# A hybrid decoder layer on one core: a new front, modulation rows as a list, and a new last output column

## The chip, the core and the metric

The kernel runs on one core of a Trainium2 chip. The metric is the device time of one execution in microseconds (us). The median of three runs of the kernel before is 730.69 us (729.06 to 731.81). The profile is that of a further execution, which took 731.29 us.

## The reference, cut to what matters

The layer takes x (512 tokens by 2048 features) and a conditioning vector c. From c it makes a modulation vector of 3 x 2048 numbers: shift, scale and gate. These two lines are what the change is about:

```python
mod = silu(c) @ w_ada + b_ada;  shift, scale, gate = split(mod, 3)
h = rms_norm(x) * (1 + scale) + shift          # 512 x 2048
proj = h @ w_in                                # 4160 columns
y = concat([rg_lru(...) * silu(gr), attention(...) * silu(ga)])
out = x + gate * (y @ w_out)                   # 2048 columns
```

All is in float32. The recurrent branch and the attention between `proj` and `y` aren't touched by the change.

## The kernel before, in words

Everything is kept with features on the 128 partitions and the 512 tokens along a row. So h is 16 tiles `h0` to `h15` of 128 x 512, one for each 128 features; the scale and the shift of a tile are a column `mod[:, 16 + k]` and a column `mod[:, k]`.

A float32 product is made of three products of rounded parts: every weight and every h is split into a high part (rounded, on ScalarE) and a low part (the rest, on VectorE), and TensorE multiplies high by high, high by low and low by high (`mm3s`, `mm_hi`, `mm_lo`; every such product is recorded at line 125). `wload` loads a group of weights and splits it into `whi` and `wlo`.

The modulation. A row of w_ada (one column of `mod` for 128 features: 128 x 2048 numbers, 1 MB) is loaded as a tile `ada`, multiplied by silu(c), which stands in every partition (`cb`), and summed along the row by one VectorE instruction (`ttr`, L276). So each h needs two such sums, of its scale row `16 + k` and of its shift row `k`, and then a multiplication by the scale and the norm (`x`, L102), the rounded h (ScalarE or L114) and its low part (L102).

The front (L220 to L465). x is loaded a second time by tokens in eight pieces of 512 KB (`xtok`) for the squares (ScalarE, `sqj`) and, through TensorE transposes, for the first two tiles of x. Ahead of the eighth piece stand the small table `vec` and the scale row of h0 (1 MB, row 16). Then the norm `rx` is made by small VectorE steps and spread over all partitions by four products on TensorE (`rb_ps`). TensorE multiplies a constant tile `junk` in between (`warm`). `make_h(0)` and `make_h(1)` follow, with their other rows in pieces of 256 or 512 KB, and the weights of the first eight output columns (`wfraw`, `wfs`), which `proj_first` multiplies: 24 products with `h0`, then 24 with `h1`.

The input projection (L528 to L546). The 16 tiles of h are cut into chunks of 2, 3, 4 and 7 (`CHUNKS`). For each of the first three chunks the loop goes over all output columns in groups of 4, 2 and 2 (`GROUP`; 128 features a column): load and split the weights, multiply, and put the sums into a `pj` tile, by ScalarE in the first chunk and added by VectorE in the others. After the first eight columns the first chunk has six groups of 24 products; the second chunk has 16 groups of 18, the third 16 of 24; a narrow column for the rotary key (`proj_kr`) stands in the middle of each. The loop draws the next chunk's h from a generator `hgen`, evenly over its groups: 6, 8 and 14 row sums in the first three chunks. A scheduler orders the instructions of VectorE, ScalarE and TensorE; the loads on SP go out in the order of the code, and each engine keeps its order.

The end. The output projection makes 16 columns of 512 tokens from 16 tiles of y in pieces of four tiles (`oproj`). The last column (`order[-1]`) is made in two halves of 256 tokens throughout, so that the first half can leave while the second is multiplied. `ofin` multiplies the sum by the gate and adds x (`xo`). The gate rows are summed by `gate`, called through `gates`.

Of the kernel before, what the change touches and what calls it, by code (L numbers as in the profile page):

```python
# [33 lines left out]
GROUP = (4, 2, 2, 1)  # L34
MORDER = tuple(range(8)) + tuple(range(20, 24)) + tuple(range(16, 20)) + tuple(range(8, 16)) + tuple(range(24, 32))
# [3 lines left out]
NB0 = 0  # L39
NB1 = 1  # L40
P0 = 8
XA = 7
SETUP = (0, 2)
WARM = (4, 6, 4, 14)
# [40 lines left out]
def body(ctx, nc, tc, a):  # L85
# [38 lines left out]
    def mm(out, lhsT, rhs, start, stop, **kw):  # L124
        PE.matmul(out=out, lhsT=lhsT, rhs=rhs, start=start, stop=stop, **kw)  # L125
# [95 lines left out]
    DMA.dma_start(out=c4, in_=a["c"])  # L221
    id4 = p1.tile([4, 4], F32, name="id4")
# [13 lines left out]
    tab(c4, c4, AF.Silu)  # L236
    split(ch, cl, c4)
# [141 lines left out]
    ada0 = [ada(16, (2, 2)), ada(0, (2, 1, 1))]  # L379
    KT0 = CHUNKS[0][1]  # L380
    NG = NF // 4
    wfs = {(k, n): bigt(4 + k * NG + n, "wfs", F32R) for k in range(KT0) for n in range(NG)}
    wfraw = {kn: pjt(16 + i, F32, "wfraw") for i, kn in enumerate(wfs)}

    def wf_load(k, n):
        raw = wfraw[k, n]
        DMA.dma_start(out=raw, in_=a["winf"][k, n])
        act(wfs[k, n][:, 0], raw, AF.Copy)
# [31 lines left out]
    warm(WARM[3])  # L420

    def make_h(k):
        if k >= KT0:
            xload(k)
        parts = (2, 2) if k < KT0 else (4,)
        if k:
            yield from ada(16 + k, parts)
        x = xt[k]
        if k == 0:
            next(ada0[1])  # L430
            next(ada0[1])
            stt(x, x, mod[:, 16:17], rb_ps, ALU.mult, ALU.mult)
            act(rb, rb_ps, AF.Copy)
            yield from ada0[1]
        else:
            yield from ada(k, parts)
            stt(x, x, mod[:, 16 + k:17 + k], rb, ALU.mult, ALU.mult)
        t = bigt(k, f"h{k}", F32R)
        hh[k], hl[k] = t[:, 0], t[:, 1]
        if k < KT0:  # L440
            ts(hh[k], x, mod[:, k:k + 1], None, ALU.add)
        else:
            act(hh[k], x, AF.Identity, bias=mod[:, k:k + 1])
        i = stt(hl[k], x, mod[:, k:k + 1], hh[k].bitcast(F32), ALU.add, ALU.subtract)
        if k < KT0:
            mark[0] = ins_of(i)

    run(make_h(0))
    wf_load(0, 1)
    los = iter(range(NG))  # L450
    for i, _ in enumerate(make_h(1)):
        if i >= NB0:
            with tc.issue_after(ins_of(ttr_last[0])):
                for n in itertools.islice(los, NB1):
                    wf_lo(0, n)
    for n in los:
        with behind():
            wf_lo(0, n)
# [4 lines left out]
    DMA.dma_start(out=row[:, :R_ID], in_=a["row"][:, :R_ID])  # L463
    DMA.dma_start(out=row[:, R_MK:], in_=a["row"][:, R_MK:])
    DMA.dma_start(out=pos_i, in_=a["pos"])  # L465
# [37 lines left out]
    def proj_first(ms):  # L503
        k0, kc = CHUNKS[0]
        ps = [bank("mm" if n < 6 else "aux", "pp") for n, m in enumerate(ms)]
        for k in range(k0, k0 + kc):
            for i, (w, h) in enumerate(((0, hh), (0, hl), (1, hh))):
                for n, m in enumerate(ms):
                    mm(ps[n], wfs[k, n // 4][:, w, (n % 4) * P:(n % 4 + 1) * P], h[k], k == k0 and i == 0, k == k0 + kc - 1 and i == 2)
        for n, m in enumerate(ms):  # L510
            evac(0, m, ps[n])
# [17 lines left out]
    for ci in range(LC):  # L529
        nk0, nkc = CHUNKS[ci + 1]  # L530
        hgen = itertools.chain.from_iterable(make_h(k) for k in range(nk0, nk0 + nkc))
        done = 0
        ng = 32 // GROUP[ci]
        g0 = NF // GROUP[ci] if ci == 0 else 0
        if ci == 0:
            proj_first(MORDER[:NF])
        for g in range(g0, ng):
            while done < 2 * nkc * (g + 1 - g0) // (ng - 1 - g0):
                next(hgen, None)
                done += 1  # L540
            if g == (g0 + ng) // 2:
                proj_kr(ci)
            proj_group(ci, g)
        run(hgen)
# [385 lines left out]
    def oproj(m, k0, k1, first, last, kind="oa"):  # L930
        halves = m == order[-1]
        if first:
            if halves:
                for i in range(2):
                    ops[m, i] = bank(kind, "oa")
            else:
                ops[m] = bank(kind, "oa")
        wh, wl = wload(a["wout"][m][:, k0 * P:k1 * P], (k1 - k0) * P)
        xs = [(yh[k], yl[k]) for k in range(k0, k1)]
        if halves:  # L940
            for i, t in enumerate(HV):
                mm3s(ops[m, i][:, t], wh, wl, [(xh[:, t], xl[:, t]) for xh, xl in xs], first, last)
        else:
            mm3s(ops[m], wh, wl, xs, first, last)
# [159 lines left out]
    for n, m in enumerate(order):  # L1104
# [3 lines left out]
        if m not in acc and m not in half:  # L1108
            ks = [(0, 4), (4, 8)] + ks
        for k0, k1 in ks:  # L1110
# [4 lines left out]
        while gated[0] < 2 * n + 2:  # L1115
            gates(32)
# [8 lines left out]
def _layout(x, c, positions, w_ada, b_ada, w_in, conv_w, conv_b, w_rg_a, b_rg_a, w_rg_x, b_rg_x, lru_lambda,  # L1125
# [6 lines left out]
    d["c"] = con(c).reshape(4, S)  # L1132
    d["pos"] = con(positions[0].reshape(NT, P).T)
# [60 lines left out]
```

## Time and profile before

| what | us |
|---|---|
| median of 3 runs | 730.69 |
| the profiled execution | 731.29 |
| its span in the trace | 729.5 |
| TensorE busy / VectorE / ScalarE | 718.4 / 527.1 / 353.6 |
| first product of h0, of h1, of the first weight group behind them | 26.79, 35.11, 40.65 |
| mean granted TensorE clock | 0.998 |

The span is from the first to the last record of the profiled execution, and 1.8 us of its time lie around it. An engine's idle time costs something only where the last work waits for it.

### The profile page before, as it was taken

Reading aid. Unit: us, or ns where it says so; the run is one execution under the profiler, and the core shown is the slowest. Engines: PE = TensorE matmul, PEld = TensorE weight load, DVE = VectorE, ACT = ScalarE, POOL = GpSimd, SP = SyncE. Lnnn points to the kernel's source line nnn. Section 1 sums busy time; section 2 is a strip of 40 time slices with the busy share of each in tenths; the row PEclk is TensorE's granted clock in tenths of the full one; section 3 lists DMA queues with packets and bytes.
Section 4 is the critical chain, followed back from the end, with each engine's and each line's share of the span. In section 5 each row is a group of like instructions: output and inputs, shape, how many; then the busy total and the mean of one; then the engine's idle time right before and its main releaser. Section 6 shows DMA issues by size and latency. Waiting matters only on the chain.

```text
span 729.5 us, 10070 instructions
## 1 busy us (share of the span) xinstructions
PE 718.4 (98%) x3625; PEld 597.0 (82%) x3626; DVE 527.1 (72%) x949; ACT 353.6 (48%) x728; POOL 29.4 (4%) x34
## 2 busy tenths in 40 slices
PE   9799999999999999999999999999999999999998
PEld 4588888788788888888888888888888887888887
DVE  2997888799998889888765566567686786783232
ACT  7376322231323479884545568677565533222221
POOL 0000000000000000001011111111120100000000
PEclk9999999999999999999999999999999999999999
DMA  8998376996922422223243315113333795984420
GB/s 306 392 404 332 116 255 224 360 329 251 355 80 55 141 91 77 76 89 102 83 134 94 90 63 202 60 58 116 130 120 132 228 297 188 312 269 166 118 93 29
DMA packets 46001, 127.94 MB, mean 175 GB/s; under 512 B 5372, under 2 KB 9340, under 8 KB 42368
## 3 DMA queue, kind: packets, MB, share of 16 engines
q1 hardware_dynamic: 38896, 106.34, 42.3%
q10 hardware_dynamic: 7056, 20.97, 8.4%
q8 instruction: 28, 0.46, 0.3%
q14 instruction: 21, 0.17, 0.1%
HBM read 123.10 MB, written 4.19 MB: 174 GB/s over the span
## 4 chain that ended last, share of the span: by engine, by line
PE 82%; DMA 8%; DVE 7%; issue 2%; SPq 1%; ACT 0%; DVEq 0%
PE pp L125 35%; PE oa L125 24%; DMA ada<-in_ada 4%; PE sc L125 4%; PE uwuv L125 3%; PE uwqn L125 3%; PE uwuk L125 3%; DVE ada L276 3%; PE op L125 2%; PE uqp L125 2%; DMA xtok<-in_xtok 1%; DVE wlo L118 1%; DVE pj L118 1%; PE tp L896 1%; DMA wfraw<-in_winf 1%
## 5 line engine op out<-in xcount | busy, mean ns | idle before, releaser
L125 PE MATMUL pp<-h,whi 128*128 128x512 f32 x992 | 241.8, 391 | 0.5 <-ACT h L90 0.5
L90 ACT ACTIVATE whi<-wraw 128x512 fp32r<-128x512 f32 (+4 forms) x172 | 126.7, 740 | 209.3 <-PE oa L125 68.4
L125 PEld LDWEIGHTS pp<-h,whi 128*128 128x128 f32 x992 | 184.9, 188 | 39.7 <-issue 0.9
L118 DVE TENSOR_TENSOR wlo<-wraw,whi 128x512 fp32r<-128x512 f32 (+4 forms) x172 | 141.0, 822 | 66.7 <-ACT whi L90 33.1
L125 PE MATMUL pp<-h,wlo 128*128 128x512 f32 x496 | 127.1, 390 | 1.0 <-DVE wlo L118 1.0
L125 PEld LDWEIGHTS pp<-h,wlo 128*128 128x128 f32 x496 | 92.8, 188 | 20.7 <-DVE wlo L118 1.5
L125 PE MATMUL oa<-yh,whi 128*128 128x512 f32 (+1 forms) x272 | 102.3, 384 | 0.1
L125 PE MATMUL oa<-yl,whi 128*128 128x512 f32 (+1 forms) x272 | 102.3, 380 | 0.0
L276 DVE CUSTOM_DVE_ANT_0 ada<-ada,cb,vec 128x2048 f32<-128x2048 f32 (+1 forms) x32 | 70.8, 2212 | 11.6 <-DMA ada<-in_ada 11.6
L118 DVE TENSOR_TENSOR pj<-pp,pj 128x512 f32<-128x512 f32 x96 | 64.0, 683 | 12.3 <-PE pp L125 11.9
L125 PE MATMUL oa<-yh,wlo 128*128 128x512 f32 (+1 forms) x272 | 71.8, 381 | 0.0
L125 PEld LDWEIGHTS oa<-yh,whi 128*128 128x128 f32 x272 | 51.3, 189 | 9.0 <-ACT yh L90 0.3
L125 PEld LDWEIGHTS oa<-yl,whi 128*128 128x128 f32 x272 | 51.3, 189 | 8.9 <-DVE yl L118 0.2
L125 PEld LDWEIGHTS oa<-yh,wlo 128*128 128x128 f32 x272 | 49.1, 189 | 9.0
L90 ACT ACTIVATE h<-x,mod 128x512 fp32r<-128x512 f32 x14 | 10.2, 730 | 32.5 <-DVE x L102 17.1
L125 PE MATMUL sc<-kT,qT 128*128 128x128 f32 (+3 forms) x96 | 22.5, 331 | 0.0
L90 ACT ACTIVATE pj<-pp 128x512 f32<-128x512 f32 x32 | 17.4, 611 | 8.9 <-PE pp L125 8.9
L229 POOL TENSOR_TENSOR hs<-hs,mhalf 128x8 f32<-128x8 f32 x12 | 21.2, 1768 | 1.0
L888 DVE TENSOR_REDUCE nm<-sc 128x1 f32<-128x128 f32 (+3 forms) x32 | 15.5, 486 | 7.9 <-PE sc L125 7.7
L90 ACT ACTIVATE pr<-sc,nm 128x128 f32<-128x128 f32 (+3 forms) x32 | 16.7, 522 | 9.2 <-DVE nm L888 9.1
L276 DVE CUSTOM_DVE_ANT_0 ada<-ada,cbo,modh 128x1024 f32<-128x1024 f32 x16 | 20.5, 1279 | 0.7 <-DMA ada<-in_ada 0.7
L125 PE MATMUL uwuv<-whi,kvt 128*128 128x256 f32 x80 | 20.8, 284 | 0.0
(222 smaller groups left out, 1005.2 us busy)
## 6 DMA issues: line engine op xcount, KB each, us to landing
ada<-in_ada SPq DMA_DIRECT2D x28, 1024.0 KB, 7.9
ada<-in_ada ACTq DMA_DIRECT2D x32, 512.0 KB, 4.9
wraw<-in_wout SPq DMA_DIRECT2D x59, 256.0 KB, 3.5
wraw<-in_win SPq DMA_DIRECT2D x22, 512.0 KB, 6.7
wraw<-in_win SPq DMA_DIRECT2D x24, 448.0 KB, 3.2
wraw<-in_win SPq DMA_DIRECT2D x16, 384.0 KB, 3.9
xtok<-in_xtok SPq DMA_DIRECT2D x8, 512.0 KB, 7.4
xo<-in_x SPq DMA_DIRECT2D x16, 256.0 KB, 5.7
```

The source lines that it names most:

```text
L90: return A.activation(out=out, in_=in_, func=func, **kw)
L118: return V.tensor_tensor(out=o, in0=x, in1=y, op=op)
L125: PE.matmul(out=out, lhsT=lhsT, rhs=rhs, start=start, stop=stop, **kw)
L229: G.tensor_tensor(out=out, in0=out, in1=mhalf[:, :n], op=ALU.pow)
L276: ttr_last[0] = V.tensor_tensor_reduce(out=t, in0=t, in1=cv, op0=ALU.mult, op1=ALU.add, scale=1.0, scalar=vec[:, C_BADA + j:C_BADA + j + 1 ...
L888: V.tensor_reduce(out=nm, in_=sp[:, :n], axis=AX.X, op=ALU.max, negate=True)
L896: PE.transpose(tp[:, j * P:(j + 1) * P], pr[:, j * P:(j + 1) * P], ident)
```

## The change

It does three things.

First, the front. All eight pieces of x are loaded first. The scale of h0 is no longer a row sum on VectorE: its 2048 x 128 weights come as 1 MB (`ada0`), and TensorE makes sixteen float32 products of 128 x 128 weights with one column of silu(c) (`ccol`), with two and six junk products behind them. The first x is multiplied by the norm before its scale is there. h0 is made in float32 (`xs`), and the eight products of the first columns with h0 take float32 operands directly, the weights as loaded; the split parts of h0 are made later, for the following groups. The second h takes x already multiplied by the norm, and ScalarE multiplies it by the scale. The small loads of `row`, the mask and the positions come behind the first chunk.

VectorE's row in the front, before, from the end of the norm (`rx`) to the first h (`ada` is a piece of a modulation row; the ISA lines are the sums and the reading of their result; x_238 is the first tile of x, h_286 the first h):

```order
L102 SCALAR_TENSOR_TENSOR rx<-tx,yx 128x4
L276 ISA ada,modh<-ada,cb,vec 128x1024
L276 ISA modh 128x1
L276 ISA ada,modh<-ada,cb,modh 128x512
L276 ISA modh 128x1
L102 SCALAR_TENSOR_TENSOR x_238<-x_238,mod,rb_ps 128x512
L276 ISA ada,mod<-ada,cb,modh 128x512
L276 ISA mod 128x1
L114 TENSOR_SCALAR h_286<-x_238,mod 128x512
L102 SCALAR_TENSOR_TENSOR h_286<-x_238,mod,h_286 128x512
```

The same place in the changed kernel (x_245 and x_247 are the first two tiles of x, `m_ps` the scale from TensorE, `xs` the float32 h0, h_298 its split form):

```order
L100 SCALAR_TENSOR_TENSOR rx<-tx,yx 128x4
L277 ISA ada,modh<-ada,cb,vec 128x1024
L277 ISA modh 128x1
L277 ISA ada,modh<-ada,cb,modh 128x512
L277 ISA modh 128x1
L116 TENSOR_TENSOR x_245<-x_245,rb_ps 128x512
L277 ISA ada,mod<-ada,cb,modh 128x512
L277 ISA mod 128x1
L116 TENSOR_TENSOR mod<-m_ps,vec 128x1
L113 TENSOR_SCALAR xs<-x_245,mod 128x512
L116 TENSOR_TENSOR x_247<-x_247,rb 128x512
L277 ISA ada,modh<-ada,cb,vec 128x1024
```

The three sums of h0's shift row stand where they stood; the scale's two sums, which stood ahead of the norm, are gone, a small addition of the scale from TensorE stands ahead of the first h, and its low part has moved back behind the next row's first sum.

Second, the rows. The generator is replaced by a list of the remaining 28 rows, worked off after each group: `row_sums` loads a row and sums it behind that group's low weights (`mark`). `AHEAD` makes the second chunk do four row sums of the third as well: 6, 12 and 10 row sums instead of 6, 8 and 14. VectorE's row in the second chunk, before, at the third and fourth group (pj tiles take the sums, 128x768 low weights are those of a group):

```order
L118 TENSOR_TENSOR wlo<-wraw,whi 128x768
L276 ISA ada,mod<-ada,cb,vec 128x2048
L276 ISA mod 128x1
L118 TENSOR_TENSOR pj_320<-pp,pj_320 128x512
L118 TENSOR_TENSOR pj_321<-pp,pj_321 128x512
L118 TENSOR_TENSOR wlo<-wraw,whi 128x768
L102 SCALAR_TENSOR_TENSOR h_974<-x_840,mod,h_974 128x512
L118 TENSOR_TENSOR pj_322<-pp,pj_322 128x512
L118 TENSOR_TENSOR pj_323<-pp,pj_323 128x512
L118 TENSOR_TENSOR wlo<-wraw,whi 128x768
```

The same stretch of the changed kernel, one group earlier:

```order
L116 TENSOR_TENSOR wlo<-wraw,whi 128x768
L277 ISA ada,mod<-ada,cb,vec 128x2048
L277 ISA mod 128x1
L116 TENSOR_TENSOR pj_327<-pp,pj_327 128x512
L116 TENSOR_TENSOR pj_328<-pp,pj_328 128x512
L116 TENSOR_TENSOR wlo<-wraw,whi 128x768
L277 ISA ada,mod<-ada,cb,vec 128x2048
L277 ISA mod 128x1
L100 SCALAR_TENSOR_TENSOR h_776<-x_740,mod,h_776 128x512
L116 TENSOR_TENSOR pj_329<-pp,pj_329 128x512
L116 TENSOR_TENSOR pj_330<-pp,pj_330 128x512
L116 TENSOR_TENSOR wlo<-wraw,whi 128x768
```

A row sum now stands behind the low weights of 12 of the groups, where it stood behind 8 of them.

Third, the last column. Its first twelve tiles of y are multiplied over all 512 tokens and put into `xo` with the gate; only the last four are multiplied in halves. The gates of a column are called ahead of its products.

The diff, cut to its core:

```diff
+AHEAD = (0, 2, 0)
-WARM = (4, 6, 4, 14)
+WARM = (4, 6, 4, 2, 6)
...
+    ccol = p1.tile([P, NK], F32, name="ccol")
+    DMA.dma_start(out=ccol, in_=a["ccol"])
+    tab(ccol, ccol, AF.Silu)
...
-        if n == XA:
-            DMA.dma_start(out=vec, in_=a["vec"])
-            ts(vec[:, 16:32], vec[:, 16:32], 1.0, None, ALU.add)
-            run(ada0[0])
         xsq(n // 2, n % 2)
-    wf_load(0, 0)
+    DMA.dma_start(out=vec, in_=a["vec"])
+    ts(vec[:, 16:32], vec[:, 16:32], 1.0, None, ALU.add)
+    m0 = [bigt(4 + q, "m0").rearrange("p k s -> p (k s)").rearrange("p (b f) -> p b f", b=8) for q in range(2)]
+    for q in range(2):
+        DMA.dma_start(out=m0[q], in_=a["ada0"][:, 8 * q:8 * q + 8])
+    run(ada(0, (2, 1, 1)))
+    for n in range(NG):
+        wf_load(0, n)
...
-    warm(WARM[3])
+    tt(xt[0], xt[0], rb_ps, ALU.mult)
+    act(rb, rb_ps, AF.Copy)
+    m0_ps = bank("mm", "m0_ps")
+    for b in range(NK):
+        i = mm(m0_ps[:, 0:1], m0[b // 8][:, b % 8], ccol[:, b:b + 1], b == 0, b == NK - 1)
+        if b % 8 == 7:
+            warm(WARM[3] if b < NK - 1 else WARM[4], i)
+    tt(mod[:, 16:17], m0_ps[:, 0:1], vec[:, 16:17], ALU.add)
...
+            if k == 0:
+                h0.append(xs)
+                mark[0] = ins_of(ts(xs, x, sc, sh, ALU.mult, ALU.add))
+                split(hh[k], hl[k], xs)
...
+            else:
+                act(xs, x, AF.Copy, scale=sc)
+                ts(hh[k], xs, sh, None, ALU.add)
+                mark[0] = ins_of(stt(hl[k], xs, sh, hh[k].bitcast(F32), ALU.add, ALU.subtract))
...
+    rows = [f + k for k in range(KT0, NK) for f in (16, 0)]
+    def row_sums(n):
+        while summed[0] < n:
+            row_load()
+            mark[0] = wlast[0]
+            j = rows[summed[0]]
+            ttr(tiles.pop(0), cb, j, True, True)
+            summed[0] += 1
+            if j < 16:
+                run(make_h(j))
...
+        for n, m in enumerate(ms):
+            mm(ps[n], wfraw[0, n // 4][:, cols(n % 4)], h0[0], True, False)
...
+        n0 = summed[0]
+        nrow = 2 * (nk0 + nkc - KT0 + AHEAD[ci]) - n0
...
+            if g < ng - 1:
+                row_sums(n0 + nrow * (g + 1 - g0) // (ng - 1 - g0))
...
-        halves = m == order[-1]
-        if first:
+        halves = last and m == order[-1]
+        if first or halves:
...
-            mm3s(ops[m], wh, wl, xs, first, last)
+            mm3s(ops[m], wh, wl, xs, first, last or (m == order[-1] and k1 == 12))
+            if m == order[-1] and k1 == 12:
+                r = xo[m // 2][:, m % 2]
+                stt(r, ops[m], mod[:, 32 + m:33 + m], r, ALU.mult, ALU.add)
```

More of the change, by code (lines that the diff above doesn't have):

```diff
@@ L1109, in body @@
             ks = [(0, 4), (4, 8)] + ks
+        while gated[0] < 2 * n + 2:
+            gates(32)
         for k0, k1 in ks:
@@ L1114, in body @@
             oload()
-        while gated[0] < 2 * n + 2:
-            gates(32)
         if m in acc:
```

87 lines of the change are left out of this document (37 added, 50 removed).

## The prediction

> **What bounds the kernel now.** I read the page's engine shares first, then the waits of TensorE, then the stages by windows.
>
> ```profile
> PE 718.4 (98%) x3625; PEld 597.0 (82%) x3626; DVE 527.1 (72%) x949; ACT 353.6 (48%) x728; POOL 29.4 (4%) x34
> PE pp L125 <- DVE h L114: 3.9, 2, 2.8
> PE pp L125 <- DVE wlo L118: 1.0, 1, 1.0
> PE pp L125 <- ACT h L90: 0.5, 1, 0.5
> 40.65:74.50 33.85, 33.85 (x150) 27.87 (x149) 27.44 (x28) 23.21 (x41) 0.00 (x0) 1.00 0.91 349
> 74.50:141.00 66.50, 65.96 (x290) 54.06 (x290) 54.21 (x69) 17.53 (x23) 0.00 (x0) 1.00 0.66 237
> 141.00:230.00 89.00, 87.97 (x389) 72.40 (x388) 84.06 (x128) 24.72 (x28) 0.00 (x0) 1.00 0.63 231
> 400.00:640.00 240.00, 239.90 (x1418) 205.93 (x1417) 163.91 (x382) 138.74 (x384) 21.37 (x20) 1.00 0.47 155
> ```
>
> The first row's 98% includes products of the constant tile junk, which compute nothing. The windows (length, then PE, weight loads, VectorE, ScalarE, GpSimd, clock) show PE full from 40.65 us on, save 0.5 us before 141 and 1.0 us behind it: the two small waits above. So only three things can move the end: when PE begins real work and how fast that goes, those two waits, and the number of PE cycles. VectorE is the next limit: 84.06 of 89 us busy in the third stage.
>
> The front, by the timeline, PE and then VectorE (start, duration, idle time before and its releaser in brackets):
>
> ```profile
> 26.79 7.23 PE L125 MATMUL pp<-h,wfs 128*128 128x512 f32 x24 [2.79 <-DVE h L114]
> 35.11 5.70 PE L125 MATMUL pp<-h,wfs 128*128 128x512 f32 x24 [1.09 <-DVE h L114]
> 40.65 1.98 PE L125 MATMUL pp<-h,whi 128*128 128x512 f32 x8
> 22.71 1.28 DVE L276 CUSTOM_DVE_ANT_0 ada<-ada,cb,vec 128x1024 f32<-128x1024 f32 x1
> 24.03 0.75 DVE L276 CUSTOM_DVE_ANT_0 ada<-ada,cb,modh 128x512 f32<-128x512 f32 x1
> 24.71 0.74 DVE L102 SCALAR_TENSOR_TENSOR x<-x,mod,rb_ps 128x512 f32<-128x512 f32 x1
> 25.37 0.74 DVE L276 CUSTOM_DVE_ANT_0 ada<-ada,cb,modh 128x512 f32<-128x512 f32 x1
> 26.16 0.49 DVE L114 TENSOR_SCALAR h<-x,mod 128x512 fp32r<-128x512 f32 x1
> 26.68 0.75 DVE L102 SCALAR_TENSOR_TENSOR h<-x,mod,h 128x512 fp32r<-128x512 f32 x1
> ```
>
> PE's real work starts at 26.79, 0.63 us behind the start of the first h on VectorE; the second row of h comes at 35.11, and the main stream at 40.65. The kernel's end is that 40.65 plus a full PE.
>
> **The front, part by part.** First the loads, which pass through one queue:
>
> ```profile
> 20.21 1.06 ACT L90 ACTIVATE sqj<-xtok 128x1024 f32<-128x1024 f32 x1 [1.23 <-DMA xtok<-in_xtok]
> 24.13 0.63 ACT L90 ACTIVATE wfs<-wfraw 128x512 fp32r<-128x512 f32 x1 [1.93 <-DMA wfraw<-in_winf]
> ```
>
> The last of x lands at 20.21, the second weight piece, 1.5 MB behind it, at 24.13: 2.61 us per MB. The change puts x ahead of 1 MB, so it lands at 20.21 - 2.61 = 17.60, and the norm, 2.50 us from there to the first shift sum in the rows (20.21 to 22.71), is ready at 20.10. The 1 MB of scale weights lands at 20.21, and the first half of the shift row 0.5 MB behind it, at 21.52. That landing decides, and the first sum starts 1.19 us earlier than 22.71. Behind it VectorE runs the same five steps, plus one small add for the scale, at most the 0.18 us by which I count it. PE starts at 26.79 - 1.19 + 0.18 = 25.78.
>
> The scale now costs PE sixteen products of one column, and h0 eight full float32 products instead of 24 split ones. The nearest rows are a one-column float32 sum (two instructions a product; it starts at 317.92, the next instruction at 318.73), four float32 products of 512, 384, 256 and 128 columns from the chain, and the split products there:
>
> ```profile
> 317.92 0.95 PE L125 MATMUL lps<-ones,lacc 128*128 128x1 f32 x8
> 318.73 1.65 PE L125 MATMUL pp<-h,wlo 128*128 128x512 f32 x6
> 447.83 2.16 PE op L125 x8
> 58.04 36.19 PE pp L125 x159
> ```
>
> So 0.101 us per small instruction, 32 of them 3.2 us, the second half behind the landing at 20.21 and the norm's broadcast: it ends near 23.8, and six junk products carry PE to 25.1, ahead of 25.78. The float32 product: 2.16 us over 2 x 1,280 columns is 0.844 ns each, so 8 x 2 x 512 columns take 6.91 us (24 split ones at 36.19/159 = 0.2276 us are 5.46). The array works longer, but nothing waits for low weights or rounding. It ends at 32.69.
>
> The second h: from h0's slot on VectorE (25.15 to 25.67) follow x times the norm (0.60), two half sums (1.21 each), the first h's low part (0.60), all from start to start below, and two dependent half sums: 1.32 as from 22.71 to 24.03, and 1.33, the 1.28 of one and the 0.05 that passed before 26.16.
>
> ```profile
> 27.34 1.28 DVE L276 CUSTOM_DVE_ANT_0 ada<-ada,cb,vec 128x1024 f32<-128x1024 f32 x1
> 28.55 0.69 DVE L118 TENSOR_TENSOR wfs<-wfraw,wfs 128x512 fp32r<-128x512 f32 x1
> 29.15 1.28 DVE L276 CUSTOM_DVE_ANT_0 ada<-ada,cb,vec 128x1024 f32<-128x1024 f32 x1
> ```
>
> 25.67 + 0.60 + 1.21 + 0.60 + 1.21 + 1.32 + 1.33 = 31.94, plus 0.63 to PE: 32.57, hidden under the float32 products by 0.12. If that cover is gone, lateness counts one for one. The second block takes 24 x 0.2276 = 5.46 and the main stream starts at 38.15 instead of 40.65: **2.50 us**. The low parts of the second weights come behind its h and are due 3.6 us into the block; they take two VectorE steps of 0.6. The row, mask and position loads now pass the six weight groups of the first chunk on SP; their first reader stands ahead of that chunk's last low weights, some 10 us early, so this is nothing, or up to 1 us if they land late.
>
> This hangs on the clock. The windows (PE busy second, clock third from the end):
>
> ```profile
> 22.00:24.00 2.00, 1.32 (x9) 0.97 (x8) 1.69 (x5) 0.20 (x1) 0.00 (x0) 1.00 1.04 413
> 24.00:26.70 2.70, 0.00 (x1) 0.00 (x0) 2.60 (x7) 1.23 (x2) 0.00 (x0) 0.98 1.01 402
> 26.70:28.00 1.30, 1.21 (x3) 1.05 (x4) 1.30 (x2) 0.00 (x0) 0.00 (x0) 0.50 1.05 393
> 28.00:30.00 2.00, 2.00 (x6) 1.52 (x6) 2.00 (x4) 0.07 (x1) 0.00 (x0) 0.50 1.09 357
> 30.00:32.00 2.00, 2.00 (x10) 1.65 (x9) 2.00 (x5) 1.20 (x2) 0.00 (x0) 0.99 1.05 416
> ```
>
> An idle 2.79 us was followed by 3.3 us at half clock. The new gap is about 0.7 us, so I take full clock. The Trainium skill, "TensorE: Matmul & The Clock Gate", section "A second HAM failure mode: psum-queue depth-cycling", says that a PE which often idles briefly between groups of products can make the gate swing. By that rule a front of one-column products between waits may run h0 cold. Here 0.68 us of idle time between 22 and 24 us left the clock at 1.00, against the rule; no run here shows one-column products in such a place.
>
> **The rows list.** It makes two rows of h (four row sums) one chunk earlier: 12 row sums in the second chunk instead of 8, and 10 in the third instead of 14. All are tied behind a group's low weights. VectorE's steps in that stage:
>
> ```profile
> 81.41 0.95 DVE L118 TENSOR_TENSOR wlo<-wraw,whi 128x768 fp32r<-128x768 f32 x1
> 82.28 0.74 DVE L102 SCALAR_TENSOR_TENSOR x<-x,mod,rb 128x512 f32<-128x512 f32 x1
> 82.94 1.28 DVE L118 TENSOR_TENSOR pj<-pp,pj 128x512 f32<-128x512 f32 x2
> 84.14 0.95 DVE L118 TENSOR_TENSOR wlo<-wraw,whi 128x768 fp32r<-128x768 f32 x1
> 85.00 2.34 DVE L276 CUSTOM_DVE_ANT_0 ada<-ada,cb,vec 128x2048 f32<-128x2048 f32 x1
> 87.27 0.08 DVE L276 DVE_READ_ACCUMULATOR2_ANT mod<- 128x1 f32 x1
> ```
>
> By start to start: low weights 0.86, x or h 0.66, two sums into pj 1.20, a row 2.27. A group with a row and an x or h takes 4.99, but PE's 18 products only 4.10. VectorE falls behind by 0.9 in most groups. From the chunk's start: low weights of group 1 end at 0.87 (they wait for the buffer). Up to those of group 15 come 14 x 2.06 + 12 x 2.27 + 11 x 0.66 + 0.87 (the key's two steps) = 64.21, so 65.08. PE needs them at 15 x 4.10 + 1.37 + 12 x 0.2276 = 65.6. Half a microsecond is left: no stall, at worst 1.5 us where ScalarE's h makes VectorE wait. The third stage then has 4 x (2.27 + 0.66) = 11.7 us less on VectorE, and the h that PE awaited at 140 is made some 20 us early. So the waits of 0.5 and 1.0 go: **1.5 us**; next late is nothing that the windows show, since the stages behind are full.
>
> **The last column.** 36 products of 512 columns replace 72 of 256, which start 0.12 apart:
>
> ```profile
> 723.23 0.28 PE L125 MATMUL oa<-yh,whi 128*128 128x256 f32 x1
> 723.35 0.28 PE L125 MATMUL oa<-yl,whi 128*128 128x256 f32 x1
> ```
>
> 72 x 0.12 - 36 x 0.2276 = **0.45 us**. The added VectorE step on xo (0.74) lies beside the first half's last 12 products (1.44). The earlier gates keep their places between the same low weights.
>
> The sum is 2.50 + 1.5 + 0.45 = 4.45 us. The profiled execution took 731.29 (729.5 of span and 1.8 around it), so it would be 726.84. It lies 0.6 above the median of 730.69, so I predict **726.3**.
>
> **Rivals.** *Cold front.* The one-column products count as idle and h0 begins at half clock. The rows show 3.3 us of that; half of it, 1.65, is lost, and the time is 727.9. For it: those products load weights and move one column. Against: eight junk products lie among them. Chance 0.18.
>
> *Part of the VectorE lag shows.* ScalarE keeps a later group's high weights ahead of an h, and VectorE waits 0.2 to 0.5 us in several groups; 1 to 3 us come back in the second chunk: 727.3 to 729.3. The half microsecond of slack speaks for it, the small ScalarE load (17.53 of 66.5) against. Chance 0.14.
>
> *The rows wait for their transfers: slower.* In the second chunk before,
>
> ```profile
> L276 DVE CUSTOM_DVE_ANT_0 ada<-ada,cb,vec 128x2048 f32<-128x2048 f32 x8 | 18.8, 2348 | 8.6 <-DMA ada<-in_ada 8.6
> ```
>
> VectorE waited 8.6 us for 8 rows, 1.08 each. Now low weights queue behind each row, so with 12 such waits 13.0 - 0.5 = 12.5 us reach PE: 726.3 + 12.5 = 738.8. It decides against the change from 0.41 us a row (4.45 + 0.5 over 12). Against it: there are three row buffers, and a transfer can start when the row three ahead is summed, over 11 us before need; the same loads landed in about 8. Chance 0.08.
>
> The forecast keeps 0.60; its own range, 725.2 to 727.8, holds an h0 up to 0.8 us late and half a microsecond of gain elsewhere. To hold 8 in 10 the range reaches over the cold front and most of the lag: 725.2 to 729.4. A measurement here can tell about 0.5%, 3.65 us, from no change: faster means under 727.04. The forecast gives 0.50 of that and 0.10 same; the cold front 0.02 and 0.16; the lag 0.02 and 0.12; the last rival 0.07 slower. Faster 0.54, same 0.38, slower 0.08.
>
> **What would show it.** In the changed profile: h0's products begin near 25.8 with the clock at 1.0, last 6.9 us, the split block follows without idle time, and the main stream starts near 38.1. PE's waits for low weights and for h are gone from 70 to 230 us, and VectorE is nearly full in the second chunk. The last 60 products take 11.1 us. Wrong would be: clock 0.50 at 26 us, PE idle ahead of the second block, PE waits on low weights late in the second chunk, or VectorE waits on rows there.

## The result, and the profile after

The changed kernel took 726.0 us (median of 17 runs, 725.03 to 730.69) against 730.84 us for the kernel before on the same chip (17 runs, 728.24 to 732.51): a ratio of 0.9944, with a 95% interval of 0.9929 to 0.9959. The forecast was 726.3. The profiled execution took 725.46 us, with a span of 723.7, which is 5.8 less than before.

Twelve of the 17 runs lie between 725.03 and 726.41 us with a mean granted clock of 0.998 to 1.000 (1 is full speed), and five between 729.11 and 730.69 with 0.993 to 0.995; the profile shown is one of the twelve, and the experiments below tell what the five most likely are.

The front of the changed kernel on TensorE, from the timeline, in the same columns as before (start, duration, operation, count):

```profile
22.36 1.84 PE L123 MATMUL m_ps<-ccol,m 128*128 128x1 f32 x16
24.06 1.46 PE L123 MATMUL junk_ps<-junk 128*128 128x512 bf16 x6
25.35 7.03 PE L123 MATMUL pp<-xs,wfraw 128*128 128x512 f32 x16
31.87 6.00 PE L123 MATMUL pp<-h,wfs 128*128 128x512 f32 x24
37.70 1.07 PE L123 MATMUL pp<-h,whi 128*128 128x512 f32 x4
```

There is no idle time in brackets any more. The scale's last sixteen small instructions end at 24.06, six constant products carry TensorE to 25.35, and h0 follows at once. The main stream starts at 37.70 instead of 40.65. VectorE at the same time:

```profile
20.02 1.28 DVE L277 CUSTOM_DVE_ANT_0 ada<-ada,cb,vec 128x1024 f32<-128x1024 f32 x1 [1.26 <-DMA ada<-in_ada]
24.24 0.16 DVE L116 TENSOR_TENSOR mod<-m_ps,vec 128x1 f32<-128x1 f32 x1 [0.82 <-PE m_ps L123]
24.43 0.55 DVE L113 TENSOR_SCALAR xs<-x,mod 128x512 f32<-128x512 f32 x1
31.24 0.49 DVE L112 TENSOR_SCALAR h<-xs,mod 128x512 fp32r<-128x512 f32 x1
```

The shift row's landing does decide first, as the prediction had it (1.26 us of waiting, at 20.02). But there is a second wait behind it: 0.82 us for the scale, which stands in TensorE's queue behind constant products. The second h starts at 31.24, and TensorE would have had it by 31.87; the float32 products begin their last instruction at 31.79 and take 0.429 each, so it is hidden by 0.35 us.

The waits of TensorE over the whole span, one row where there were more:

```profile
PE junk_ps L123 <- DVE spe L356: 1.6, 1, 1.6
```

Only a wait at the very start is left. The waits for low weights and for h are gone. The second chunk, VectorE's row sums grouped by form, and then the last group's low weights with the TensorE products that need them:

```profile
L277 DVE CUSTOM_DVE_ANT_0 ada<-ada,cb,vec 128x2048 f32<-128x2048 f32 x12 | 28.2, 2350 | 0.0
```

```profile
136.86 0.96 DVE L116 TENSOR_TENSOR wlo<-wraw,whi 128x768 fp32r<-128x768 f32 x1
```

```profile
140.16 1.52 PE L123 MATMUL pp<-h,wlo 128*128 128x512 f32 x6
```

All twelve row sums ran with no wait for a transfer (8.6 us for eight of them before). The low weights are ready at 137.82 and needed at 140.16, 2.3 us later. From the start of the main stream to the same fourteen products of the fourth chunk (258.76 before, 253.50 after) it is 218.11 us before and 215.80 after: 2.31 us less. This is the figure of one pair of executions. In the three other profiles below that have the old rows (e10_xfirst, e9_beforewarm, e9b) the same stretch takes 217.01 to 219.60 us, and in the nine that have the list with at most two h made ahead 215.56 to 215.83, so the rows are worth 1.2 to 3.8 us, depending on the execution.

The last column, its first product and its last four before, and then the changed kernel's first product, first half-width product and last four:

```profile
714.60 0.28 PE L125 MATMUL oa<-yh,whi 128*128 128x256 f32 x1
725.63 0.64 PE L125 MATMUL oa<-yh,wlo 128*128 128x256 f32 x4
```

```profile
709.22 0.39 PE L123 MATMUL oa<-yh,whi 128*128 128x512 f32 x1
717.38 0.28 PE L123 MATMUL oa<-yh,whi 128*128 128x256 f32 x1
719.77 0.64 PE L123 MATMUL oa<-yh,wlo 128*128 128x256 f32 x4
```

Thirty-six products of 512 columns take 8.16 us and are followed by 24 of 256. The last four start 10.55 us behind the column's first product, and 11.03 before: 0.48 us less. So the 5.8 us of span are 2.95 in front, 2.31 from the main stream to the fourth chunk, 0.48 at the end, and less than 0.1 between. The medians lie only 4.84 us apart, since the profile before took 0.45 us more than its median and the one after 0.54 less.

### The profile page after: what moved, and what is told of

It is laid out like the page before. It is cut to its first block, busy times and chain, and to the rows that moved or that the text cites. A ratio compares the mean times of both kernels' runs of the same rounds, so it can differ in the third digit from the quotient of the medians.

```text
span 723.7 us, 10053 instructions
## 1 busy us (share of the span) xinstructions
PE 718.7 (99%) x3608; PEld 596.0 (82%) x3608; DVE 525.6 (73%) x945; ACT 354.2 (49%) x729; POOL 29.4 (4%) x34
## 4 chain that ended last, share of the span: by engine, by line
PE 99%; DVE 0%; ACT 0%; issue 0%
PE pp L123 48%; PE oa L123 24%; PE sc L123 4%; PE uwuv L123 3%; PE uwqn L123 3%; PE uwuk L123 3%; PE op L123 2%; PE junk_ps L123 2%; PE uqp L123 2%; PE tp L926 1%; PE pk L123 1%; PE tq L826 1%; PE pi L123 1%; PE pr L123 1%; PE tqe L881 0%; PE m_ps L123 0%
## 5 line engine op out<-in xcount | busy, mean ns | idle before, releaser
L123 PEld LDWEIGHTS oa<-yl,whi 128*128 128x128 f32 x260 | 49.0, 188 | 9.3 <-DVE yl L116 0.2
L123 PEld LDWEIGHTS oa<-yh,whi 128*128 128x128 f32 x260 | 48.9, 188 | 9.4 <-ACT yh L88 0.3
L123 PE MATMUL uwqn<-whi,kvt 128*128 128x256 f32 x80 | 20.7, 286 | 0.0
L277 DVE CUSTOM_DVE_ANT_0 ada<-ada,cbo,modh 128x1024 f32<-128x1024 f32 x16 | 20.5, 1281 | 0.0
L277 DVE CUSTOM_DVE_ANT_0 ada<-ada,cbo,vec 128x1024 f32<-128x1024 f32 x16 | 20.5, 1280 | 0.0
```

The source lines that it names most:

```text
L123: return PE.matmul(out=out, lhsT=lhsT, rhs=rhs, start=start, stop=stop, **kw)
L277: ttr_last[0] = V.tensor_tensor_reduce(out=t, in0=t, in1=cv, op0=ALU.mult, op1=ALU.add, scale=1.0, scalar=vec[:, C_BADA + j:C_BADA + j + 1 ...
```

## The experiments

A time of one execution varies by some microseconds here, in part because the first loads do. The squares of x's last piece on ScalarE started at 16.1 to 17.9 us in eleven profiles with x first, and at 20.21, 20.15 and 18.23 in three with the old order. In these three ScalarE waited for the load, so the mark is its landing; in the eleven it came from earlier work without a wait, and the piece had landed before. So the effects are read from marks in each profile. "Rest" is the span, which is given to a tenth of a microsecond, less the main stream's start.

| run | squares of x's last piece | h0's products | second h on VectorE | main stream | rest |
|---|---|---|---|---|---|
| before | 20.21 | 26.79 | 34.48 | 40.65 | 688.85 |
| after | 16.17 | 25.35 | 31.24 | 37.70 | 686.00 |
| e1_oldcol | 17.47 | 25.54 | 31.69 | 37.95 | 686.45 |
| e2_noahead | 16.23 | 24.54 | 30.44 | 36.89 | 687.61 |
| e2c_ahead1 | 17.00 | 25.08 | 31.23 | 37.51 | 685.89 |
| e2b_ahead4 | 16.85 | 24.93 | 31.08 | 37.35 | 692.75 |
| e3_nojunk | 17.85 | 25.94 | 32.09 | 41.03 | 685.97 |
| e4_split | 16.69 | 25.38 | 32.00 | 38.12 | 685.98 |
| e6_scaledve | 16.11 | 24.72 | 30.91 | 39.61 | 685.89 |
| e6w | 16.52 | 24.92 | 31.12 | 37.36 | 686.14 |
| e5b | 17.71 | 31.25 | 33.16 | 43.60 | 685.90 |
| e9_beforewarm | 20.15 | 27.80 | 35.49 | 43.23 | 689.87 |
| e9b | 18.23 | 24.82 | 32.51 | 38.69 | 690.31 |
| e10_xfirst | 17.57 | 26.19 | 33.88 | 40.07 | 687.73 |

**The last column alone.** The edit of the changed kernel:

```diff
-        halves = last and m == order[-1]
-        if first or halves:
+        halves = m == order[-1]
+        if first:
...
-            mm3s(ops[m], wh, wl, xs, first, last or (m == order[-1] and k1 == 12))
...
+            mm3s(ops[m], wh, wl, xs, first, last)
```

> The changed kernel with the last column as it was before: halves of 256 tokens over all sixteen tiles of y. Theory (product count): 72 products of 256 columns, 0.12 apart, come back for 36 of 512 at 0.2276, so the last column alone grows by 0.45 us, the main stream still starts at 37.7, and a single execution takes about 725.9. Rival (the sums and the gate behind the first twelve tiles hold something up, so part of the gain of halves is eaten): the column is as long as it is now or shorter, a difference of 0.2 us or less.

It took 726.15 us. The rest is 686.45 against 686.00, and from the column's first product to its last four it is 11.03 us against 10.55: 0.48, so the theory of the product count holds.

**The rows, with none, one and four h made ahead.** Before, VectorE worked off 8 rows in the second chunk and 14 in the third.

```diff
-AHEAD = (0, 2, 0)
+AHEAD = (0, 0, 0)
```

> The changed kernel with AHEAD at 0, 0, 0: the list, tied behind low weights, but 6, 8 and 14 row sums in the chunks as before. Theory A (the two rows of h made a chunk earlier remove the waits): the third chunk's VectorE is again as full as before (84.06 of 89 us), and TensorE's gaps on h and low weights, about 2.3 us in all between the main stream's start and the end of the third chunk, come back for the most part: 1.5 to 2.3 us longer there. Theory B (the list itself removes them: rows tied behind low weights and spread over the groups): by VectorE's steps a group of the third chunk takes 5.70 against TensorE's 24 x 0.2269 = 5.445, a lag of some 3.6 us at its end that the slack covers, so TensorE waits less than 0.5 us in all and the time is within 0.5 us of the changed kernel's.

It took 726.29 us, and the rest is 1.61 longer. But both theories had the place wrong. The second and the third chunk have no wait at all, so the list tied behind the low weights is enough for these. The 1.6 us stand in the fourth chunk, ahead of the key, where the kernel before has no wait:

```profile
317.27 1.78 PE L123 MATMUL pp<-h,wlo 128*128 128x512 f32 x7
320.57 3.49 PE L123 MATMUL pk<-h,wkhl 128*128 128x512 f32 x14 [1.52 <-DVE wkhl L116]
```

VectorE made the key's low weights at 319.90 here and at 316.97 in the changed kernel. In this kernel the rows kept the tables of the positions out of the third chunk (the tables were still being made at 234 us, where they were done by 225), and VectorE was busy for 77.2 of 85 us from 225 to 310 us instead of 75.3. That its arrears were handed on to the key is the likely reason; the order of VectorE's steps in the fourth chunk differs too, and the runs don't part the two. So of the 2.31 us the list alone would have kept 0.7. With one h ahead:

```diff
-AHEAD = (0, 2, 0)
+AHEAD = (0, 1, 0)
```

> The changed kernel with AHEAD at 0, 1, 0: 10 row sums in the second chunk and 12 in the third. With 8 and 14 TensorE waited 1.7 us once, for the key's low weights in the fourth chunk, and with 12 and 10 nowhere. Theory (two rows fewer in the third chunk are enough for VectorE to hand over no arrears): no wait above 0.3 us from the main stream to the end of the fourth chunk's key, within 0.2 us of the changed kernel over that stretch. Rival (each row of h left in the third chunk costs): 0.5 to 1.0 us of waits there.

It took 725.21 us. The rest is 685.89 and no wait above 0.2 us is left up to the fourth chunk's key, so one h ahead does what two do. With four (16 rows in the second chunk):

```diff
-AHEAD = (0, 2, 0)
+AHEAD = (0, 4, 0)
```

> The changed kernel with AHEAD at 0, 4, 0: 16 row sums in the second chunk and 6 in the third. This measures VectorE's slack in the second chunk, which I put at half a microsecond and which now reads 2.3. Theory (VectorE's lag adds up): four more rows and two more x and h steps are 4 x 2.27 + 4 x 0.66 = 11.7 us more VectorE work, so the low weights of the last group end at 66.3 + 11.7 = 78.0 after the chunk's start against 68.7 needed, and TensorE waits 6 to 10 us on low weights in the second chunk; time about 732 to 735. Rival (VectorE has more room than the sums of steps say): less than 2 us of waits.

It took 731.92 us, and the rest is 6.75 us longer: the theory holds, in the lower part of its range. The wait comes in another place than it said, at the sums that free TensorE's output tiles (`pj`) as much as at weights. Three neighbouring groups of the second chunk on TensorE:

```profile
120.62 3.00 PE L123 MATMUL pp<-h,whi 128*128 128x512 f32 x12 [0.57 <-DVE pj L116]
125.62 3.00 PE L123 MATMUL pp<-h,whi 128*128 128x512 f32 x12 [0.64 <-DVE pj L116]
130.62 3.00 PE L123 MATMUL pp<-h,whi 128*128 128x512 f32 x12 [0.64 <-ACT h L88]
```

The groups are 5.00 us apart where 18 products take 4.10: VectorE's sum of steps, 4.99, has become the pace. Which releaser is named changes from group to group, while the pace doesn't.

**The constant products among the one-column products.** Two stand between them and six behind:

```diff
-WARM = (4, 6, 4, 2, 6)
+WARM = (4, 6, 4, 0, 0)
```

> The changed kernel without the eight junk products among and behind the sixteen one-column products. They took about 1.8 us of TensorE's queue ahead of the scale sum's end. Theory (one-column products keep the clock): the clock stays at 1.00 at h0; the scale is ready earlier, and the main stream starts at about 36.9 instead of 37.7. Rival (the cold front of the prediction: one-column products count as idle): the clock shows 0.50 from h0's first product on for some 3 us, the float32 products take 1.6 us longer, and the main stream starts at about 38.5.

It took 728.74 us; the rival holds, and at a higher price than it named. TensorE, then the windows (length, PE, weight loads, VectorE, ScalarE, GpSimd, clock, DMA), and one of a microsecond (length, PE, clock, DMA):

```profile
22.07 2.07 PE L123 MATMUL m_ps<-ccol,m 128*128 128x1 f32 x18
25.94 9.77 PE L123 MATMUL pp<-xs,wfraw 128*128 128x512 f32 x16 [1.81 <-ACT rb L88]
41.03 1.07 PE L123 MATMUL pp<-h,whi 128*128 128x512 f32 x4
```

```profile
20.00:25.00 5.00, 4.13 (x38) 4.05 (x37) 3.51 (x9) 1.27 (x3) 0.00 (x0) 0.95 1.05 400
25.00:30.00 5.00, 4.06 (x5) 1.85 (x6) 4.96 (x11) 1.29 (x3) 0.00 (x0) 0.50 1.03 401
30.00:35.00 5.00, 5.00 (x11) 2.11 (x10) 4.82 (x9) 2.53 (x4) 0.00 (x0) 0.87 1.04 418
```

```profile
24.00:25.00 1.00, 0.13 (x2) 0.74 1.03 401
```

With a clock of either 1.0 or 0.5, a mean c over a length L stands for 2(1 - c)L of half clock: 0.5 + 5.0 + 1.3 = 6.8 us. By the last row it began at 24.48, and TensorE had been busy until 24.13. So the clock fell 0.35 us behind the last one-column product; the 3 us before were 2.07 us of one-column products and the broadcast's eight of 128 columns. In e9_beforewarm below, with constant products ahead, TensorE idled for 3.7 us (18.76 to 22.44) until the clock fell. So the small products didn't hold the clock up. The block of h0, from its start to 5.46 us (the second block) ahead of the main stream, lasts 9.63 us instead of 6.89: 2.7 us lost. The h0 products themselves start only 0.6 later than in the changed kernel, with x 1.7 later.

**Fewer constant products ahead of the one-column products, and more behind them.** The changed kernel's VectorE waited 0.82 us for the scale, so I thinned the constant products in TensorE's queue ahead of it (the second number stands behind each of the eight pieces of x, the third behind the norm's first steps, the last two between and behind the one-column products):

```diff
-WARM = (4, 6, 4, 2, 6)
+WARM = (4, 4, 0, 0, 16)
```

> The changed kernel with the constant products moved: 4 fewer ahead of and 2 fewer between the one-column products, 16 instead of 6 behind them. Theory (in the changed kernel's profile VectorE waited 0.82 us for the scale from TensorE, whose queue held constant products ahead of it): that wait goes, h0 comes up to 0.8 us earlier, at 24.5, and is bound by VectorE; the main stream starts at 36.6 to 37.0. Rival (a landing or the second h binds there at once): main stream at 37.5 or later. In time this is at most 0.8 of 726, which the rounds can hardly tell from nothing; the profile decides. It goes wrong if the clock falls, since the one-column products then stand alone for 4 us: main stream at 39 to 41.

The edit takes away more than this says: sixteen constant products behind the pieces of x go as well, so the kernel has 52 of them instead of 64. It went wrong in the last of the ways named, and worse: 731.68 us (12 runs, 729.01 to 733.05), a ratio to before of 1.0002 (0.9987 to 1.0017). The whole gain of the change is gone. TensorE and a window:

```profile
18.41 5.15 PE L123 MATMUL m_ps<-ccol,m 128*128 128x1 f32 x28 [2.44 <-DMA m<-in_ada]
25.98 5.43 PE L123 MATMUL junk_ps<-junk 128*128 128x512 bf16 x16
31.25 7.03 PE L123 MATMUL pp<-xs,wfraw 128*128 128x512 f32 x16
43.60 1.07 PE L123 MATMUL pp<-h,whi 128*128 128x512 f32 x4
```

```profile
20.00:25.00 5.00, 5.00 (x24) 5.00 (x25) 3.07 (x8) 0.00 (x0) 0.00 (x0) 0.50 1.05 401
```

From 20 to 25 us TensorE counts as busy for all of 5.00 us, up to 23.43 with one-column products and then with the broadcast's eight of 128 columns, and the clock stays at 0.50. It had fallen at 19.5, and came back at 29.7, 3.7 us after the first wide constant product. Why it fell isn't shown here, since the thinned queue left TensorE idle for 2.44 us ahead of these products; but they don't raise it, and in e3_nojunk they didn't hold it up. At half clock they also last longer (0.213 us from start to start from 20.23 to 22.36, against 0.106 for the sixteen above), VectorE waits 1.76 us for the norm's broadcast behind them, and the sixteen constant products, now too many, hold h0 until 31.25 though `xs` was started at 26.36.

**The scale on VectorE, behind x.** The sixteen products and their constant products go, and the row is summed:

```diff
-    m0 = [bigt(4 + q, "m0").rearrange("p k s -> p (k s)").rearrange("p (b f) -> p b f", b=8) for q in range(2)]
-    for q in range(2):
-        DMA.dma_start(out=m0[q], in_=a["ada0"][:, 8 * q:8 * q + 8])
+    run(ada(16, (2, 2)))
...
-    m0_ps = bank("mm", "m0_ps")
-    for b in range(NK):
-        i = mm(m0_ps[:, 0:1], m0[b // 8][:, b % 8], ccol[:, b:b + 1], b == 0, b == NK - 1)
-        if b % 8 == 7:
-            warm(WARM[3] if b < NK - 1 else WARM[4], i)
-    tt(mod[:, 16:17], m0_ps[:, 0:1], vec[:, 16:17], ALU.add)
```

> The changed kernel with the scale of h0 back as two row sums on VectorE, behind x in the queue; the sixteen one-column products and their junk are gone. Theory (the scale on TensorE pays for itself): two sums of 1.28 us come ahead of h0 on VectorE, TensorE's work before h0 ends some 3 us ahead of it, the clock falls to 0.50 as it did before, h0 starts near 26.5 and the main stream at 39.2 to 39.8, 1.5 to 2 us later than now. Rival (x first does it all, the scale's place does not matter): main stream at 37.7 to 38.2.

It took 727.26 us.

```profile
24.72 9.57 PE L123 MATMUL pp<-xs,wfraw 128*128 128x512 f32 x16 [2.91 <-DVE xs L113]
39.61 1.07 PE L123 MATMUL pp<-h,whi 128*128 128x512 f32 x4
```

The main stream starts where the theory had it, but not for its first reason. The two sums hardly delayed h0: it starts 8.6 us behind the squares of x's last piece, against 9.2 in the changed kernel's profile and 8.1 to 8.3 in the four with the same front (e1 and the three e2). VectorE had the time while the shift row was on its way. The loss is the clock: its mark of 0.50 lasts 6.8 us again, and h0's block 9.43 instead of 6.89. So the next kernel fills TensorE's queue, and nothing else:

```diff
-WARM = (4, 6, 4, 2, 6)
+WARM = (4, 6, 10, 13)
...
-        mm(rb_ps[:, cols(i)], rx[:, i:i + 1].broadcast_to([P, P]), ident, True, True)
+        rbi = mm(rb_ps[:, cols(i)], rx[:, i:i + 1].broadcast_to([P, P]), ident, True, True)
+    warm(WARM[3], rbi)
```

> The kernel with h0's scale as two row sums on VectorE behind x, with TensorE now kept busy by constant products: 12 instead of 6 ahead of the norm's broadcast, 13 tied behind it (13 x 0.216 = 2.8 us, to about 24.5). Without them this kernel had h0 0.6 us earlier than the changed kernel (24.72 against 25.35) and a clock of 0.50 from 23 to 29 us, which made its eight float32 products last 9.0 us. Theory (sixteen products on TensorE buy nothing but a filled queue; VectorE had idle time for the scale's two sums): the clock stays at 1.00, h0 starts at 24.7, the float32 products take 6.87, and the main stream starts at 24.7 + 6.87 + 5.46 = 37.0, so as early as the changed kernel's or up to 0.7 earlier; 726 within the spread of the measurement. Rival (VectorE's two sums push the norm and the second h later): main stream at 38 or later, with TensorE idle ahead of the second h.

It took 725.54 us (6 runs, 725.07 to 726.97), a ratio to before of 0.9928 (0.9909 to 0.9947).

```profile
22.06 2.97 PE L123 MATMUL junk_ps<-junk 128*128 128x512 bf16 x13
24.92 7.13 PE L123 MATMUL pp<-xs,wfraw 128*128 128x512 f32 x16
37.36 1.07 PE L123 MATMUL pp<-h,whi 128*128 128x512 f32 x4
```

The clock is 1.00 and the main stream starts 0.34 earlier than in the changed kernel, with x 0.35 later. The theory holds: the scale on TensorE is worth little here that constant products don't give as well. From the squares of x's last piece to the main stream it is 20.84 us, against 21.53 in the changed kernel's profile and 20.5 to 20.7 in the four with its front, so 0.4 us at most. The intervals of the two kernels overlap, so this one isn't shown to be faster. All six of its runs have a mean clock of 0.998 to 1.000, where five of the changed kernel's 17 don't; if it failed as often, six good runs in a row would still come once in eight times, so this isn't shown to be steadier either. A clock of 0.995 over 724 us is 7.2 us of half clock, about as in e3_nojunk and e6_scaledve, which have the same 0.995; 0.993, which two of the five have, is 10.1 us, as in e5b. So these five runs are most likely fronts that went cold; no trace of one was taken.

**h0 split instead of float32.** The first eight columns take 24 products with h0 again:

```diff
+    for n in range(NG):
+        with behind():
+            wf_lo(0, n)
...
-        for n, m in enumerate(ms):
-            mm(ps[n], wfraw[0, n // 4][:, cols(n % 4)], h0[0], True, False)
-        for k in range(k0 + 1, k0 + kc):
+        for k in range(k0, k0 + kc):
...
```

> The changed kernel with h0's first columns in 24 split products (rounded and low weights) instead of eight float32 ones. Theory (what float32 gives is the steps that it takes off VectorE): the low weights of two groups, 0.6 us each, and the low part of h0 stand again ahead of the second h; TensorE's work at h0 shrinks from 6.8 to 5.46 us, but the second h comes at 32.4 or later, so TensorE stands idle 1.5 us ahead of it and the main stream starts at about 38.5, 0.8 later than now. Rival (the float32 products only cost their 1.4 us more array time): no idle time, main stream at 36.3.

It took 725.87 us.

```profile
25.38 2.14 PE L123 MATMUL pp<-h,wfs 128*128 128x512 f32 x8 [0.36 <-ACT h L88]
28.33 3.91 PE L123 MATMUL pp<-h,wfs 128*128 128x512 f32 x16 [0.81 <-DVE h L116]
32.54 5.74 PE L123 MATMUL pp<-h,wfs 128*128 128x512 f32 x24 [0.31 <-DVE h L112]
38.12 1.07 PE L123 MATMUL pp<-h,whi 128*128 128x512 f32 x4
```

The theory holds: TensorE's shorter work turns into 1.48 us of waits, for h0's rounding on ScalarE, its low part on VectorE and the second h. In the two profiles in which the shift row landed alike (its first sum at 20.65 here, at 20.81 in e2b_ahead4), the main stream comes at 38.12 and 37.35, so float32 is worth about 0.8 us.

**The kernel before: the order of the loads, and the half clock.** First all of x ahead of the table and the scale row:

```diff
-        if n == XA:
-            DMA.dma_start(out=vec, in_=a["vec"])
-            ts(vec[:, 16:32], vec[:, 16:32], 1.0, None, ALU.add)
-            run(ada0[0])
...
+    DMA.dma_start(out=vec, in_=a["vec"])
+    ts(vec[:, 16:32], vec[:, 16:32], 1.0, None, ALU.add)
+    run(ada0[0])
```

> The kernel before with all eight pieces of x loaded ahead of the small table and h0's scale row; the scale stays two row sums on VectorE, everything else is as before. Theory (the landing of x bounds the norm, but the scale's sums now come behind it): x lands 2.6 us earlier, of which the two scale sums, 2.6 us, take a part where VectorE would have stood idle; h0 and the main stream come 0.5 to 1.5 us earlier than before, at 39.2 to 40.2. Rival (order alone is worth the whole front): main stream at 38 or earlier. Rival on the other side: the scale sums come right behind the norm's wait and the main stream is no earlier than 40.65.

It took 729.59 us; the main stream starts at 40.07. x came 2.64 us earlier and the main stream 0.58: the two scale sums now stand behind x on VectorE and take the rest, and the clock is 0.50 at h0 as before. The theory holds. The rest is another 1.12 us shorter than in the profile before, by smaller waits for weights and h behind the front; that the order of the first loads brings this isn't shown, since this stretch varies between executions.

Then constant products behind the norm's broadcast. In the first attempt I took the 14 of before from where they were:

```diff
-WARM = (4, 6, 4, 14)
+WARM = (4, 6, 4, 12)
...
-    warm(WARM[3])
+    warm(WARM[3], rbi)
```

> The kernel before with its junk products (12 instead of 14) tied behind the norm's broadcast, so that TensorE is busy until about 26.6 and the idle 2.79 us ahead of h0 goes. Nothing else changes. Theory (the cold clock of before cost nothing, since the second h decided): h0's block runs at full clock and ends some 1.8 us earlier, TensorE waits that much longer for the second h, and the main stream still starts at 40.65 plus or minus 0.2. Rival (the warm clock is a part of the 2.95 us won in front): main stream near 39.0.

It took 734.91 us and doesn't answer the question cleanly: TensorE stood idle for 4.04 us ahead of the broadcast, which then ran at half clock and held VectorE for 0.97. Still, h0's block ran at full clock, and the second h's products started 8.32 us behind h0's, exactly as before (26.79 to 35.11). The repeat leaves the 14 and adds 12:

```diff
-WARM = (4, 6, 4, 14)
+WARM = (4, 6, 4, 14, 12)
...
     warm(WARM[3])
+    warm(WARM[4], rbi)
```

> The kernel before with all of its constant products left where they were and 12 more tied behind the norm's broadcast, so that only the idle 2.79 us ahead of h0 is filled. Theory (the second h decides in the kernel before; the half clock only filled the time until it came): h0 starts at 26.8 at full clock, its 24 products end near 32.3, TensorE is idle 2 to 3 us until the second h at 35.1, and the main stream is no earlier than before: 40.65, or later, near 42.2, if the clock falls in that new idle time. Rival (the warm clock is by itself part of what the change won in front): main stream near 39.0.

It took 730.78 us. TensorE:

```profile
24.82 4.78 PE L125 MATMUL pp<-h,wfs 128*128 128x512 f32 x20
30.33 1.20 PE L125 MATMUL pp<-h,wfs 128*128 128x512 f32 x4 [0.74 <-DVE wfs L118]
33.13 5.72 PE L125 MATMUL pp<-h,wfs 128*128 128x512 f32 x24 [1.60 <-DVE h L114]
38.69 1.98 PE L125 MATMUL pp<-h,whi 128*128 128x512 f32 x8
```

The clock is 1.00 throughout, and h0's products wait for low weights and the second h instead. The main stream's 38.69 looks like the rival's 39.0, but in this execution x came 2 us early; from the squares of its last piece to the main stream it is 20.46 us, and 20.44 before. So the half clock in the kernel before cost nothing, and the same half clock in e6_scaledve cost 2.5 (9.43 against 6.89): it is free where the second h decides, and dear once VectorE's path to that h is shorter.

## Why the prediction was right, step by step

*The front (2.50 forecast, 2.95 in the profile).* The mechanism held: the shift row's landing decides first, the float32 block takes 6.91 (6.89), the second h is hidden (by 0.35, not 0.12), the second block follows without a gap. In e1_oldcol, e2b_ahead4 and e2c_ahead1 the row's first sum starts at 20.81 to 21.42, and h0 follows it by 4.12 us with no wait for the scale, where the forecast had 4.26. The mis-sized step is the landing of that row at 21.52. In the eight profiles with the same first loads its first sum, which waits for it, starts at 20.02 to 21.83, and the profile shown has the earliest. The forecast took one execution's landing as fixed. With the row 1.5 us early, TensorE's own queue decided h0's start, at 25.35. The forecast had that queue's end at 25.1 and called it out of the way. The step before it, "lands at 17.60", isn't tested: with x first the squares started without a wait for the load, at 16.17 in the profile. That the means of this mark lie 2.61 apart (16.92 in eleven profiles, 19.53 in three), the forecast's figure, is chance, since the three alone spread over 2 us.

*What of the change earns it.* x first alone gave 0.58 (e10_xfirst). The rest comes from VectorE's shorter path from h0 to the second h (6.8 us from `xs` to it in e6w, 8.3 in e10_xfirst), which needs the float32 products, and from a clock that stays up. The scale on TensorE gave 0.4 us of its own at most.

*The clock (full, forecast).* Right for the profile and for twelve of 17 runs. But my argument, that eight constant products lie among the one-column ones, was thinner than its 0.18 for a cold front says: without those eight the front is cold, and it most likely was in five of 17 runs (0.29). The rival's price of 1.65 us came from half of 3.3 us, one spell of half clock. The spells here lasted 3.4 us in the kernel before, 6.8 in e3_nojunk and e6_scaledve and 10.2 in e5b, and cost 2.5 to 2.7 and, in e5b, all of the gain. The Trainium skill, "TensorE: Matmul & The Clock Gate", section "Part 1: The HAM clock gate (the "warmup" mystery)", says that the gate judges free-running windows of about 3.4 us. By that rule spells come in whole windows, and these do: one, two and three.

*The rows (1.5 forecast, 2.31).* The waits went, and the rival of waiting for transfers showed nothing: 0.0 us for twelve rows. Two sizes were off. The waits of before were taken as 0.5 and 1.0 from the view of waits, which counts idle time from modelled ends; from start to start they are 0.24 + 0.70 + 0.10 in the second chunk and 1.20 + 0.13 in the third. And the slack of "half a microsecond" was 2.3: VectorE was about as late as forecast (66.3 us against 65.1 from the chunk's start), but TensorE's order puts 16 products of the next chunk ahead of that need. And the forecast credited the wrong part. It had the waits go because four row sums, 11.7 us of VectorE's work, leave the third chunk; but with none made ahead they go all the same, so the list tied behind the low weights removes them. What the rows ahead remove is a wait of 1.6 us in the fourth chunk, which the kernel before doesn't have and the forecast didn't see.

*The last column (0.45 forecast, 0.48).* Right, and 0.48 when undone alone.

*The sum (726.3 forecast, 726.0).* It is nearer than its terms, and that is luck. Front and rows came out 0.45 and 0.81 us better in the profile, each in a term that varies by 2 us or more between executions, and the profile after happens to lie 0.54 below its median. The five runs that most likely went cold lift the median to 726.0; the other twelve have 725.82. Two slips changed little: 726.84 less 0.60 is 726.24, and the chances of slower add up to 0.07.

## What to carry to other kernels

Work on an engine that seems to waste its time can be what holds its clock: before moving or removing filler, or putting small products in its place, look at the granted clock of the stretch behind it, and don't count on one-column products to hold it. A faster clock or a shorter transfer earns only what the next path leaves: here the half clock was free until VectorE's path to the second h had been cut. And a term that rests on when a load lands needs several executions, since one profile gives it to no better than 2 us here.

## What the runs showed of the hardware

TensorE was busy for all of 5 us with float32 products of one and of 128 columns, and its clock stayed at half: 0.213 us from one small instruction to the next then, against 0.106 at full clock. A float32 product of 512 columns is two instructions of 0.429 us, and a split one of 512 columns starts every 0.2276, so three split products (0.68) beat one float32 product (0.86) on TensorE alone, by 1.4 us over eight; the float32 form won by about 0.8 because h0's rounding and the low parts no longer stand in the way.
